# One PSUM bank for each partial product of a pair, down weights split ahead of the next pair's, turns one round later

## The chip, the cores and the metric

The kernel runs on one NeuronCore of a Trainium2 chip. The core has five engines that run side by side and meet at semaphores: TensorE (PE) multiplies matrices into PSUM, VectorE (DVE) and ScalarE (ACT) work on SBUF and PSUM, GpSimd (POOL) works on SBUF and issues some DMAs, SyncE (SP) issues most DMAs. PEld is PE's weight load, which overlaps its matmuls. Sixteen DMA engines move data between the main memory and SBUF.

The metric is the device time of one execution in microseconds (us).

## The reference

One layer of a diffusion backbone for 128 context tokens and 512 latent tokens, `D_MODEL` 1024, all in float32: modulation from a conditioning vector, RMS norm, one input projection shared by three mixers (neighbourhood attention, gated DeltaNet, gated linear attention), their merge and output projection, and a gated MLP with a centred convolution of width 3. The change touches the MLP alone:

```python
h2 = rms_norm(x, n2) * (1 + sc2) + sh2
u_val, u_gate = jnp.split(dw_conv(h2 @ w_up, f_conv), 2, axis=-1)
x = x + gt2 * ((jax.nn.silu(u_gate) * u_val) @ w_dn)
```

`w_up` is 1024 x 5632 and `w_dn` 2816 x 1024. The convolution doesn't cross from the latent to the context tokens.

## The kernel before, in words

Activations lie with features on the 128 partitions and the 640 tokens (T) side by side. A float32 matrix product is made of three passes: each operand is split into a high part (an ACT cast, L149 for weights, L402 for activations) and a low part (a DVE subtraction, L150 and L403), and high x high, high x low and low x high are added up in PSUM. `wh` and `wl` are rings of two tiles (`WB`), `whd` and `wld` for the down weights too; the raw weights that DMAs bring have a ring of three (`RAWB`), the raw down weights (`rawd`) of two.

PSUM is in three pools: `g`, two tiles of 1024 float32 a partition, two banks each (`gtile`); `m` and `s`, two tiles of 512, one bank each (`mtile`, `stile`).

The MLP's 22 hidden tiles of 128 features (f) come in six blocks of 4, 4, 4, 4, 3 and 3. The first block's are made plainly by `up_tile`: a value product (uv) and a gate product (ug), 48 matmuls of 320 columns each into a g tile, a convolution (`conv`: a centre tap on ACT, L510, and four side taps on DVE, L512), SiLU, a product, and a split into `ac[f]`. uv 0, ug 0 and uv 1 are made early, ahead of the normalisation. `sums_h2(k)` makes sums and differences of the activations' halves, which are split too (`hs`).

The other 18 tiles are made by `up_pair`. It makes value and gate together in the manner of Strassen and Winograd: the 2 x 2 block product (two halves of the input features, value and gate, two halves of the tokens, L and R) takes 7 products of 12 matmuls instead of 8. They build up in three partial sums, X, Y and Z, in the order X, Y, Z, X, Y, Z, Y. X and Y are the two banks of one g tile, Z is an s tile. Between two products into it, X is copied out by ACT (L1725 and L1741), and Y and Z are read by DVE (L1730, L1735, L1750, L1753, L1757).

The weights of a pair are four tiles, `("st", f, 0)` to `("st", f, 3)`. Some are sums of weight blocks: POOL's DMAs add one block onto another in the raw tile (L250), and DVE adds two raw tiles (`st_sums`, L264 for tile 0 and L267 for tile 2). L264 for the next pair needs both the next pair's weight 1 with its addition landed and the next pair's weight 0.

Behind each pair come two or three down projections of the block before (`down`): 24 matmuls (18 for a block of three) each, into g tiles, whose result DVE adds to the residual (L1782, two instructions). The down projections of the last block stand at the end, each followed by its turn: five transposes on PE (L617) into s tiles, two copies on ACT (L1790), two DMAs out on SP.

What sets the order: the stage of pairs and downs is under `tc.manual_schedule` for DVE, ACT and PE, so these engines run its instructions in the order in which the program issues them. Ahead of it, and on SP and POOL, a planner orders the instructions by readiness and priority. `W(key)` hands out a weight's split; for plain weights it loads two and splits one ahead (`LOOK_L`, `LOOK_S`), whatever the kind of the next. `need_split` and `need_load` issue a split or a load at their place.

At the end of a pair before the change the splits stand in this order: the first down weight's ahead of the last product; behind it the sum and split of the next pair's weight 0, the second down weight's split, and, ahead of the last down projection, that of the next pair's weight 1:

```python
        for i, key in enumerate(dn):
            if i == 0:
                st_sums(f + 1, 0)
                need_split(("st", f + 1, 0))
            if i + 1 < len(dn):
                need_split(dn[i + 1])
```

Of the kernel before, what the change touches and what calls it, by code (L numbers as in the profile page):

```python
# [18 lines left out]
P = 128  # L19
D = 1024  # L20
KT = 8
TS = 512
TP = 128
T = TS + TP
# [34 lines left out]
def hybrid_step(ctx: ExitStack, tc: tile.TileContext, a: dict, o: list):  # L59
# [18 lines left out]
    def gtile():  # L78
        return psg.tile([P, 1024], F32, tag="g", name=nm("g"))
# [4 lines left out]
    def stile():  # L84
        return psm.tile([P, 512], F32, tag="s", name=nm("s"))

    def body(ps):
        return ps[:, OFF:OFF + T]
# [197 lines left out]
    def need_split(key):  # L286
        j = pidx.get(key)
        if j is not None and j not in split:
            need_load(key)
            split[j] = split_of(j)  # L290

    def W(key):
        i = pidx[key]
        assert i == used[0], (key, i, used[0])
        used[0] += 1
        if key[0] in ("st", "wd"):
            need_split(key)
            return split[i]
        with tc.high_priority() if i else nullcontext():
            for j in range(i, min(i + LOOK_L + 1, len(plan))):  # L300
                if j not in loaded:
                    loaded[j] = load_of(j)
            for j in range(i, min(i + LOOK_S + 1, len(plan))):
                if j not in split:
                    split[j] = split_of(j)
        return split[i]

# [64 lines left out]
    def gemm_b(*args, **kw):  # L372
        for _ in gemm_p(*args, **kw):
            pass
# [1278 lines left out]
    def gated(f, uv, ug):  # L1653
# [3 lines left out]
        ac[f] = rt(2)  # L1657
        split_x(uv, *(t[:, :T] for t in ac[f]))

    def up_tile(f):  # L1660
        ys = {}

        for key, f2 in sorted((("uv", f), ("ug", NF + f)), key=lambda i: (i[0], f) in early):
            ys[key] = ft()
            if (key, f) in early:
                src = early[key, f]
            else:
                ps = gtile()
                gemm_b(ps, W((key, f)), lambda k: h2H[:, k, :], lambda k: h2L[:, k, :], KT)
                src = body(ps)  # L1670
            conv(ys[key], src, lambda tap, f2=f2: fcols[:, tap, f2:f2 + 1])
            if (key, f) in early:
                fslots.append(early[key, f])
        gated(f, ys["uv"], ys["ug"])
        fslots.extend(ys.values())

    L, R = slice(0, HALF), slice(HALF, T)
    hs = {}  # L1680

    def sums_h2(k):
# [21 lines left out]
    def up_pair(f, dn):  # L1704


        ps = gtile()
        X, Y, Z = ps[:, :HALF], ps[:, 512:512 + HALF], stile()[:, :HALF]

        def prod(out, w, kh, xx, start, stop):  # L1710

# [39 lines left out]
        prod(Z, w, 1, lambda j, k: hH2[j][:, 4 + k, R], False, True)  # L1751
        need_split(dn[0])
        V.tensor_add(u1[:, R], u1[:, R], Z)  # L1753
        w = W(("st", f, 3))
        prod(Y, w, 0, lambda j, k: hs[k, 1][j][:, L], False, True)
        open_["prev"] = f, conv_u(u1, f), u2
        V.tensor_sub(u2[:, L], Y, u2[:, L])  # L1757
        for i, key in enumerate(dn):
            if i == 0:
                st_sums(f + 1, 0)  # L1760
                need_split(("st", f + 1, 0))
            if i + 1 < len(dn):
                need_split(dn[i + 1])
            if i == len(dn) - 1:
                need_split(("st", f + 1, 1))
            down(*key[1:])
            need_load(*wds[wds.index(key) + 2:wds.index(key) + 3])
# [6 lines left out]
    def down(b, nt):  # L1774
        ps = gtile()
        if b == NB_F - 1:
            for n in (nt, nt + 1):
                need_split(("wd", b, n))
            need_load(("wd", b, nt + 2))
        gemm_b(ps, W(("wd", b, nt)), lambda k: ac[fst[b] + k][0], lambda k: ac[fst[b] + k][1], FBLK[b])  # L1780
        for r, (c0, c1) in enumerate(((0, TS), (TS, T))):
            V.scalar_tensor_tensor(out=x1[nt][:, c0:c1], in0=body(ps)[:, c0:c1], scalar=modc[:, 40 + nt, r:r + 1],  # L1782
                                   in1=x1[nt][:, c0:c1], op0=ALU.mult, op1=ALU.add)
        if nt == 7:
            for k in range(FBLK[b]):
                slots.extend(ac.pop(fst[b] + k))
        if b == NB_F - 1:
            yt_ = ft()
            yt = chunks(yt_)
            tr_chunks(x1[nt], lambda c0, n, v: S.copy(yt[:, c0:c0 + n, :], v))  # L1790
            ns_ = slice(nt * P, (nt + 1) * P)
            SY.dma_start(out=y_s[0, :, ns_].rearrange("(c p) d -> p c d", p=P), in_=yt[:, 0:4, :])
            SY.dma_start(out=y_p[0, :, ns_], in_=yt[:, 4, :])
            fslots.append(yt_)

    up_tile(1)
    up_tile(2)
    sums_h2(0)
    sums_h2(1)
    up_tile(0)  # L1800
    up_tile(3)
    sums_h2(2)
    sums_h2(3)
    e1x.close()
    e2 = ctx.enter_context(tc.tile_pool(name="e2", bufs=1, reuse_waits="tile"))
    slots.extend(e2.tile([P, T + 2], F32R, name=f"r{i}") for i in range(24, 32))
    with tc.manual_schedule(engines={nc.vector.engine, nc.scalar.engine, nc.tensor.engine}):
        need_load(*wds[:2])
        for b in range(1, NB_F):
            for i in range(FBLK[b]):  # L1810
                up_pair(fst[b] + i, [("wd", b - 1, nt) for nt in downs(b, i)])
        last_gate()
        for nt in range(8):
            down(NB_F - 1, nt)


# [32 lines left out]
```

## Time and profile before

| | |
|---|---|
| median of 3 runs | 1477.54 us (1476.49 to 1483.48) |
| profiled execution | 1470.56 us |
| its span, first to last instruction | 1468.3 us |
| PE busy | 1340.4 us (91%) |
| PEld busy | 1253.7 us (85%) |
| DVE busy | 900.4 us (61%) |
| ACT busy | 574.6 us (39%) |
| POOL busy | 218.1 us (15%) |
| mean granted TensorE clock | 0.972 of full speed |
| DMA | 137.96 MB, mean 94 GB/s |

All times in profile rows are of the one profiled execution, counted from its first instruction. A row of a group gives busy time, the mean duration of one instruction in ns, and the idle time of the engine just before such instructions with what ended most of it. A row in order of time gives start, duration, engine, line and operation, the tile written and those read (buffer numbers left out), and in brackets how long the engine had stood idle and what it waited for. Matmuls are pipelined, so the distance between two starts tells more than a duration. The up tiles run from about 936 to 979 us, the 18 pairs from 979.6, the last block's down projections from 1427.3.

### The profile page before, as it was taken

How to read it: one execution, taken by the hardware profiler on the slowest of the kernel's cores; microseconds unless marked ns; L12 is line 12 of the kernel's file. 1: busy time of each engine (PE TensorE's matmuls, PEld its weight loads, DVE VectorE, ACT ScalarE, POOL GpSimd, SP SyncE). 2: the span in 40 equal slices, each digit the busy share in tenths (PEclk: the TensorE clock that was granted, in tenths of full speed). 3: DMA queues.
4: the chain of work that ended last, by engine and by line, in shares of the span. 5: the costliest groups of instructions: out<-in, count | busy, mean ns of one | idle time of the engine just before them, and what ended most of it. 6: DMA issues, size and time to landing. Idle time of an engine off the chain costs nothing.

```text
span 1468.3 us, 27024 instructions
## 1 busy us (share of the span) xinstructions
PE 1340.4 (91%) x10985; PEld 1253.7 (85%) x10985; DVE 900.4 (61%) x1863; ACT 574.6 (39%) x1080; POOL 218.1 (15%) x224
## 2 busy tenths in 40 slices
PE   5999999998888999999999999888888898989886
PEld 4899999998777889999988989878888888888776
DVE  4775876676887543443433355886676666667663
ACT  4543334323855322343333245743333333332322
POOL 1011022212334110121200221001010101010100
PEclk9999999999999999999999999989999999999999
DMA  9524330331011344434445253115353444343413
GB/s 276 144 58 99 92 74 23 79 91 37 20 49 32 69 106 110 121 92 107 119 144 165 80 154 91 56 37 117 78 117 91 103 102 100 98 105 83 103 45 94
DMA packets 228078, 137.96 MB, mean 94 GB/s; under 512 B 22037, under 2 KB 221491, under 8 KB 227955
## 3 DMA queue, kind: packets, MB, share of 16 engines
q1 hardware_dynamic: 208563, 126.48, 31.5%
q0 software_dynamic: 19008, 9.44, 5.3%
q8 instruction: 86, 1.41, 0.4%
q14 instruction: 37, 0.30, 0.1%
q10 hardware_dynamic: 384, 0.33, 0.1%
HBM read 129.67 MB, written 6.55 MB: 93 GB/s over the span
## 4 chain that ended last, share of the span: by engine, by line
PE 61%; DVE 14%; ACT 6%; issue 4%; POOL 3%; DMA 1%; ACTq 0%; SPq 0%; DVEq 0%; POOLq 0%
PE g L369 34%; PE g L1714 9%; PE s L1714 4%; DVE t L512 3%; PE g L390 2%; ACT wh L149 2%; PE s L617 1%; DVE wl L150 1%; PE s L417 1%; PE s L1443 1%; ACT t L510 1%; DVE wld L150 1%; PE s L1431 1%; DVE raw L264 1%; POOL ssn L339 1%
## 5 line engine op out<-in xcount | busy, mean ns | idle before, releaser
L150 DVE TENSOR_TENSOR wl<-raw,wh 128x1024 fp32r<-128x1024 f32 (+1 forms) x176 | 193.6, 1100 | 193.5 <-ACT wh L149 182.5
L149 ACT CAST wh<-raw 128x1024 fp32r<-128x1024 f32 (+1 forms) x176 | 166.3, 945 | 343.7 <-PE g L369 176.5
L369 PE MATMUL g<-hH,wh 128*128 128x320 f32 x768 | 186.4, 322 | 3.0 <-DVE xb L725 1.5
L369 PE MATMUL g<-hL,wh 128*128 128x320 f32 x768 | 183.5, 317 | 0.6 <-DVE hL L465 0.6
L369 PE MATMUL g<-hH,wl 128*128 128x320 f32 x768 | 182.7, 316 | 0.0
L369 PE MATMUL g<-r,whd 128*128 128x320 f32 x704 | 145.4, 332 | 26.3 <-ACT whd L149 26.3
L369 PEld LDWEIGHTS g<-r,whd 128*128 128x128 f32 x704 | 120.1, 205 | 31.1 <-ACT whd L149 31.0
L369 PEld LDWEIGHTS g<-hH,wh 128*128 128x128 f32 x768 | 129.2, 191 | 11.2 <-issue 3.9
L369 PEld LDWEIGHTS g<-hL,wh 128*128 128x128 f32 x768 | 130.2, 190 | 3.4 <-issue 1.8
L369 PEld LDWEIGHTS g<-hH,wl 128*128 128x128 f32 x768 | 131.0, 191 | 2.2 <-issue 1.9
L1714 PE MATMUL g<-r,wh 128*128 128x320 f32 x432 | 100.3, 319 | 22.7 <-ACT t L1741 9.3
L250 POOL DMA_DIRECT2D raw<-in_w_up_dram x36 | 46.4, 1290 | 420.8 <-DMA raw<-in_w_up_dram 183.2
L1714 PEld LDWEIGHTS g<-r,wh 128*128 128x128 f32 x432 | 71.2, 188 | 32.8 <-ACT t L1741 14.0
L390 PE MATMUL g<-wh,hH 128*128 128x256 f32 x320 | 94.4, 295 | 3.4 <-DVE xb L725 3.4
L369 PE MATMUL g<-r,wld 128*128 128x320 f32 x352 | 88.1, 334 | 8.3 <-DVE wld L150 8.3
L512 DVE SCALAR_TENSOR_TENSOR t<-t,fcols,t 128x511 f32<-128x511 f32 (+1 forms) x156 | 82.2, 548 | 19.8 <-ACT t L510 17.3
L390 PE MATMUL g<-wl,hH 128*128 128x256 f32 x320 | 93.9, 293 | 0.0
L390 PE MATMUL g<-wh,hL 128*128 128x256 f32 x320 | 93.8, 293 | 0.0
L1782 DVE SCALAR_TENSOR_TENSOR xa<-g,modc,xa 128x512 f32<-128x512 f32 x96 | 48.3, 545 | 53.7 <-PE g L369 53.7
L369 PE MATMUL g<-oz,wh 128*128 128x320 f32 x384 | 73.8, 314 | 1.3 <-DVE xb L1304 1.2
L369 PEld LDWEIGHTS g<-r,wld 128*128 128x128 f32 x352 | 64.1, 206 | 12.7 <-DVE wld L150 12.7
L390 PEld LDWEIGHTS g<-wh,hH 128*128 128x128 f32 x320 | 62.6, 196 | 5.2 <-DVE xb L725 3.6
(594 smaller groups left out, 2912.4 us busy)
## 6 DMA issues: line engine op xcount, KB each, us to landing
raw<-in_w_in_dram SPq DMA_DIRECT2D x64, 512.0 KB
raw<-in_w_up_dram SPq DMA_DIRECT2D x90, 256.0 KB
wada<-in_w_ada_dram SPq DMA_DIRECT2D x32, 512.0 KB
raw<-in_w_up_dram POOLq DMA_DIRECT2D x36, 256.0 KB, 4.7
wat<-in_w_ada_dram SPq DMA_DIRECT2D x16, 512.0 KB
rawd<-in_w_down_dram SPq DMA_DIRECT2D x32, 256.0 KB
raw<-in_w_branch_dram SPq DMA_DIRECT2D x24, 256.0 KB
raw<-in_w_out_dram SPq DMA_DIRECT2D x8, 512.0 KB
```

Of the source, the lines that this page charges most:

```text
L149: S.copy(wh[:, :m], raw[:, :m])
L150: V.tensor_sub(wl[:, :m], raw[:, :m], wh[:, :m].bitcast(F32))
L250: G.dma_start(out=lo, in_=part(1, 2 - j), accum_op=ALU.add)
L264: V.tensor_add(st_raw[f, 0][:, 512:], st_raw[f, 0][:, :512], st_raw[f, 1][:, :512])
L339: G.tensor_tensor(out=out, in0=out, in1=mh.broadcast_to([P, n]), op=ALU.pow)
L369: PE.matmul(out=ps[:, OFF + c0:OFF + c1], lhsT=ww[:, k, :], rhs=xx(k)[:, c0:c1], start=(k == 0 and i == 0), stop=(k == kt - 1 and i == 2))
L390: PE.matmul(out=ps[b][:, o:o + GRP], lhsT=xx[:, 4 * kh + k, cs], rhs=ww[:, k, :], start=(kh == 0 and c % 2 == 0 and k == 0 and i == 0), st ...
L417: PE.matmul(out=pa[32 * g:32 * g + 32, :w], lhsT=csil[:, k, :], rhs=t[g], start=start, stop=stop)
L510: S.activation(out=y, in_=src, func=AF.Copy, scale=w3(1))
L512: V.scalar_tensor_tensor(out=y[:, o0:o1], in0=src[:, i0:i0 + o1 - o0], scalar=w3(t), in1=y[:, o0:o1], op0=ALU.mult, op1=ALU.add)
L1714: PE.matmul(out=out, lhsT=ww[:, 4 * kh + k, :], rhs=xx(hl_, k), start=start and k == 0 and i == 0, stop=stop and k == 3 and i == 2, skip_g ...
L1782: V.scalar_tensor_tensor(out=x1[nt][:, c0:c1], in0=body(ps)[:, c0:c1], scalar=modc[:, 40 + nt, r:r + 1], in1=x1[nt][:, c0:c1], op0=ALU.mul ...
```

## The change

X and Y of a pair become two m tiles, one bank each; g tiles are left to the down projections. The split of the second down weight is issued ahead of the pair's last product, and later down weights ahead of the next pair's. ug 2 is computed into two m tiles, half of the tokens each, and copied by ACT into an SBUF tile, from which its convolution reads. `W` no longer splits a pair's weight ahead; the split of `("st", 4, 0)` is issued behind ug 3's product. The order of up tiles and sums is changed, so that up tile 0 (whose products are early) stands last. The turns of the last block are a function of their own, issued one down projection later.

```diff
--- before.py
+++ after.py
@@ -301,7 +301,7 @@
                 if j not in loaded:
                     loaded[j] = load_of(j)
             for j in range(i, min(i + LOOK_S + 1, len(plan))):
-                if j not in split:
+                if j not in split and plan[j][0][0] != "st":
                     split[j] = split_of(j)
         return split[i]
 
@@ -1657,6 +1657,8 @@
         ac[f] = rt(2)
         split_x(uv, *(t[:, :T] for t in ac[f]))
 
+    L, R = slice(0, HALF), slice(HALF, T)
+
     def up_tile(f):
         ys = {}
 
@@ -1665,9 +1667,25 @@
             if (key, f) in early:
                 src = early[key, f]
             else:
-                ps = gtile()
-                gemm_b(ps, W((key, f)), lambda k: h2H[:, k, :], lambda k: h2L[:, k, :], KT)
-                src = body(ps)
+                w = W((key, f))
+                if (key, f) == ("ug", 2):
+
+                    ps = mtile(), mtile()
+                    for k in range(KT):
+                        for i, (ww, xx) in enumerate(((w[0], h2H), (w[0], h2L), (w[1], h2H))):
+                            for p_, cs in zip(ps, (L, R)):
+                                PE.matmul(out=p_[:, :HALF], lhsT=ww[:, k, :], rhs=xx[:, k, cs],
+                                          start=(k == 0 and i == 0), stop=(k == KT - 1 and i == 2))
+                    src = ft()
+                    for p_, cs in zip(ps, (L, R)):
+                        S.copy(src[:, cs], p_[:, :HALF])
+                    early[key, f] = src
+                else:
+                    ps = gtile()
+                    gemm_b(ps, w, lambda k: h2H[:, k, :], lambda k: h2L[:, k, :], KT)
+                    src = body(ps)
+                if (key, f) == ("ug", 3):
+                    need_split(("st", f + 1, 0))
             conv(ys[key], src, lambda tap, f2=f2: fcols[:, tap, f2:f2 + 1])
             if (key, f) in early:
                 fslots.append(early[key, f])
@@ -1676,7 +1694,6 @@
 
 
 
-    L, R = slice(0, HALF), slice(HALF, T)
     hs = {}
 
     def sums_h2(k):
@@ -1704,8 +1721,7 @@
     def up_pair(f, dn):
 
 
-        ps = gtile()
-        X, Y, Z = ps[:, :HALF], ps[:, 512:512 + HALF], stile()[:, :HALF]
+        X, Y, Z = mtile()[:, :HALF], mtile()[:, :HALF], stile()[:, :HALF]
 
         def prod(out, w, kh, xx, start, stop):
 
@@ -1751,16 +1767,17 @@
         prod(Z, w, 1, lambda j, k: hH2[j][:, 4 + k, R], False, True)
         need_split(dn[0])
         V.tensor_add(u1[:, R], u1[:, R], Z)
+        need_split(dn[1])
         w = W(("st", f, 3))
         prod(Y, w, 0, lambda j, k: hs[k, 1][j][:, L], False, True)
         open_["prev"] = f, conv_u(u1, f), u2
         V.tensor_sub(u2[:, L], Y, u2[:, L])
         for i, key in enumerate(dn):
+            if i + 1 < len(dn):
+                need_split(dn[i + 1])
             if i == 0:
                 st_sums(f + 1, 0)
                 need_split(("st", f + 1, 0))
-            if i + 1 < len(dn):
-                need_split(dn[i + 1])
             if i == len(dn) - 1:
                 need_split(("st", f + 1, 1))
             down(*key[1:])
@@ -1784,23 +1801,24 @@
         if nt == 7:
             for k in range(FBLK[b]):
                 slots.extend(ac.pop(fst[b] + k))
-        if b == NB_F - 1:
-            yt_ = ft()
-            yt = chunks(yt_)
-            tr_chunks(x1[nt], lambda c0, n, v: S.copy(yt[:, c0:c0 + n, :], v))
-            ns_ = slice(nt * P, (nt + 1) * P)
-            SY.dma_start(out=y_s[0, :, ns_].rearrange("(c p) d -> p c d", p=P), in_=yt[:, 0:4, :])
-            SY.dma_start(out=y_p[0, :, ns_], in_=yt[:, 4, :])
-            fslots.append(yt_)
+
+    def turn_out(nt):
+        yt_ = ft()
+        yt = chunks(yt_)
+        tr_chunks(x1[nt], lambda c0, n, v: S.copy(yt[:, c0:c0 + n, :], v))
+        ns_ = slice(nt * P, (nt + 1) * P)
+        SY.dma_start(out=y_s[0, :, ns_].rearrange("(c p) d -> p c d", p=P), in_=yt[:, 0:4, :])
+        SY.dma_start(out=y_p[0, :, ns_], in_=yt[:, 4, :])
+        fslots.append(yt_)
 
     up_tile(1)
+    sums_h2(0)
     up_tile(2)
-    sums_h2(0)
     sums_h2(1)
+    sums_h2(2)
+    up_tile(3)
+    sums_h2(3)
     up_tile(0)
-    up_tile(3)
-    sums_h2(2)
-    sums_h2(3)
     e1x.close()
     e2 = ctx.enter_context(tc.tile_pool(name="e2", bufs=1, reuse_waits="tile"))
     slots.extend(e2.tile([P, T + 2], F32R, name=f"r{i}") for i in range(24, 32))
@@ -1812,6 +1830,9 @@
         last_gate()
         for nt in range(8):
             down(NB_F - 1, nt)
+            if nt:
+                turn_out(nt - 1)
+        turn_out(7)
 
 
 # ---- launch: one core; inputs and outputs as the reference has them ----
```

## Rows read from the trace of the kernel before

**Rows 1.** The page of the kernel before: its first line, and from its part 4 (the chain of work that ended last) the shares of the span by engine.

```profile
span 1468.3 us, 27024 instructions
...
PE 61%; DVE 14%; ACT 6%; issue 4%; POOL 3%; DMA 1%; ACTq 0%; SPq 0%; DVEq 0%; POOLq 0%
```

**Rows 2.** The table by stretch: start and end in us, length, then busy us (and instructions) of PE, PEld (weight load), DVE, ACT and POOL, the granted TensorE clock, the share of the DMA engines and GB/s. The stretches are the first pair, the next eleven, the next three, the next two, the last pair with its down projections, and seven of the eight rounds at the end.

```profile
979.50:1009.50 30.00, 23.18 (x132) 21.56 (x133) 20.96 (x34) 11.79 (x17) 2.56 (x2) 0.89 0.36 79
1009.50:1273.50 264.00, 235.15 (x1454) 223.62 (x1453) 181.65 (x297) 91.11 (x132) 28.24 (x22) 0.95 0.45 99
1273.50:1351.10 77.60, 69.71 (x447) 66.57 (x446) 52.73 (x87) 25.89 (x38) 7.72 (x6) 0.98 0.43 97
1351.10:1399.20 48.10, 41.39 (x260) 39.30 (x259) 33.95 (x57) 16.54 (x25) 5.14 (x4) 0.96 0.44 98
1399.20:1421.00 21.80, 20.77 (x140) 20.19 (x138) 14.75 (x27) 6.57 (x11) 0.00 (x0) 1.00 0.14 40
...
1433.30:1463.50 30.20, 23.63 (x162) 22.03 (x162) 10.52 (x21) 7.75 (x20) 0.00 (x0) 1.00 0.37 103
```

**Rows 3.** What PE's matmuls waited for in the whole pair stage, 979 to 1413 us, each wait over 1 us in total: waiting engine, what it writes, line, what it waited for, us in total, times, longest.

```profile
PE g L369 <- ACT whd L149: 20.3, 17, 1.9
PE g L1714 <- ACT t L1741: 9.3, 18, 0.5
PE g L1714 <- ACT t L1725: 9.3, 18, 0.5
PE g L369 <- DVE wld L150: 8.3, 17, 0.5
PE g L1714 <- ACT r L402: 3.6, 1, 3.6
```

**Rows 4.** PE in order of time in one pair (start us, us, engine, line, operation, out<-in, shape, how many were merged, and in brackets the idle time before with what ended it): first matmul of X; first of Y after the copy of X; first and last matmul of X's second half; first of Y after the second copy; first of the first down projection; first of the second; its first with the low part; first matmul of the next pair.

```profile
1153.81 0.31 PE L1714 MATMUL g<-h2H,wh 128*128 128x320 f32 x1
...
1156.25 0.56 PE L1714 MATMUL g<-r,wh 128*128 128x320 f32 x2 [0.52 <-ACT t L1725]
...
1159.88 0.31 PE L1714 MATMUL g<-h2H,wh 128*128 128x320 f32 x1
...
1161.49 0.31 PE L1714 MATMUL g<-h2H,wl 128*128 128x320 f32 x1
1162.32 0.56 PE L1714 MATMUL g<-r,wh 128*128 128x320 f32 x2 [0.52 <-ACT t L1741]
...
1167.69 0.74 PE L369 MATMUL g<-r,whd 128*128 128x320 f32 x4
...
1172.46 0.85 PE L369 MATMUL g<-r,whd 128*128 128x320 f32 x4 [1.11 <-ACT whd L149]
1173.81 0.56 PE L369 MATMUL g<-r,wld 128*128 128x320 f32 x2 [0.49 <-DVE wld L150]
...
1176.83 0.31 PE L1714 MATMUL g<-h2H,wh 128*128 128x320 f32 x1
```

**Rows 5.** DVE in order of time in the same pair: the convolution of the pair before (L512), the second sum of weights (L267), the low part of weight 2, the convolution of this pair, the sum for the next pair (L264), the low part of the next pair's weight 0, the low part of the second down weight, and the result of the first down projection (L1782).

```profile
1154.94 2.18 DVE L512 SCALAR_TENSOR_TENSOR t<-t,fcols,t 128x511 f32<-128x511 f32 x4
1157.03 0.68 DVE L267 TENSOR_TENSOR raw<-raw,raw 128x512 f32<-128x512 f32 x1
...
1159.30 1.23 DVE L150 TENSOR_TENSOR wl<-raw,wh 128x1024 fp32r<-128x1024 f32 x1 [0.42 <-ACT wh L149]
...
1167.58 2.19 DVE L512 SCALAR_TENSOR_TENSOR t<-t,fcols,t 128x511 f32<-128x511 f32 x4 [0.96 <-ACT t L510]
...
1170.08 0.68 DVE L264 TENSOR_TENSOR raw<-raw,raw 128x512 f32<-128x512 f32 x1
1171.92 1.23 DVE L150 TENSOR_TENSOR wl<-raw,wh 128x1024 fp32r<-128x1024 f32 x1 [1.16 <-ACT wh L149]
1173.07 0.68 DVE L150 TENSOR_TENSOR wld<-rawd,whd 128x512 fp32r<-128x512 f32 x1
1173.67 1.00 DVE L1782 SCALAR_TENSOR_TENSOR xa<-g,modc,xa 128x512 f32<-128x512 f32 x2
```

**Rows 6.** ACT in order of time in the same pair: the copy of X, the centre tap of the convolution (L510), the cast of the next pair's weight 0, the cast of the second down weight.

```profile
1155.78 0.42 ACT L1725 COPY t<-g 128x320 f32<-128x320 f32 x1 [6.25 <-PE g L1714]
...
1166.71 0.83 ACT L510 ACTIVATE t<-t,fcols 128x640 f32<-128x640 f32 x1 [2.79 <-DVE t L1753]
1170.84 1.05 ACT L149 CAST wh<-raw 128x1024 fp32r<-128x1024 f32 x1 [3.30 <-DVE raw L264]
1171.80 0.61 ACT L149 CAST whd<-rawd 128x512 fp32r<-128x512 f32 x1
```

**Rows 7.** POOL and SP's queue in order of time in the same pair, the DMA that adds onto the next pair's weight 1 and the two loads of down weights (a merged row runs from the first issue to the end of the last); and, from the answer on line L250 in the whole stage, the time from issue to landing of its 34 additions.

```profile
1164.04 1.29 POOL L250 DMA_DIRECT2D raw<-in_w_up_dram  x1 [20.38 <-DVE wl L150]
...
1165.50 8.65 SPq L140 DMA_DIRECT2D rawd<-in_w_down_dram  x2
...
DMA to landing us min/median/max: 4.3/4.7/6.2
```

**Rows 8.** PE in order of time among the up tiles: the first matmul of ug2.

```profile
954.39 0.53 PE L369 MATMUL g<-h2H,wh 128*128 128x320 f32 x2 [4.25 <-DVE t L512]
```

**Rows 9.** DVE's waits from 950 to 992 us: the sum of weights for the first pair, which waited once.

```profile
DVE raw L264 <- DMA raw<-in_w_up_dram: 3.1, 1, 3.1
```

**Rows 10.** PE's groups from 1433.3 to 1463.5 us (busy us, mean ns of one, idle before and what ended it): the transposes of the turns.

```profile
L617 PE MATMUL s<-ident,xa 128*128 128x128 f32 x36 | 5.5, 280 | 7.4 <-DVE xa L1782 7.4
```

## The prediction

> **What bounds the kernel now.** I read the page first: the chain that ended last is 61% TensorE (PE), more than four times any other engine, in a span of 1468.3 us [rows 1]. So a cost counts where PE stands still. The table by stretch came next. In the eleven pairs from 1009.5 to 1273.5 PE is granted 0.95 of its clock and the DMA engines are used to 0.45; VectorE (DVE) works 181.65 of 264.0 us [rows 2]. Then the waits of PE for the whole pair stage: 20.3 us for the cast of a down weight (whd), 8.3 us for its low part (wld), and twice 9.3 us for ScalarE's (ACT's) copies at L1725 and L1741, eighteen times each [rows 3]. Last, one pair in order of time.
>
> In that pair a product of 12 matmuls runs at 1.61/11 = 0.1464 us a matmul (1159.88 to 1161.49), and the pair takes 1176.83 - 1153.81 = 23.02 us. It needs 7 x 12 + 2 x 24 = 132 matmuls, 19.3 us. The rest is four stops: each copy leaves 0.83 us between matmuls instead of 0.15 (1161.49 to 1162.32) and a slower first double (0.56), 0.78 us in all; the second down projection waits 1.11 us for whd and 0.49 us for wld, about 2.1 us with two restarts [rows 4]. [...]
>
> **The change part by part.**
>
> *X and Y in banks of their own.* Y's matmuls write other columns than the copy of X reads, yet they start only when the copy ends (0.52 us after PE ran dry, [rows 4]); from 1162.32 to 1167.69 three products, one of them in Z's own tile, run 36 matmuls in 5.37 us without a stop. So I take the wait to be one for the shared tile, and the new tiles to end it: 2 x 0.78 us a pair. What Y still needs (its own weights, the sums) is ready: rows 3, which holds every wait of PE over 1 us, has none for a wl. The m tiles come round once a pair; the last reader of the old Y is the subtraction just ahead of 1170.08 [rows 5], 6.7 us before the next X.
>
> *Down weights split earlier.* Now whd of the second down projection follows the cast of the next pair's first weight (1170.84), which waits 3.30 us for the sum L264, which waits for the convolution on DVE [rows 5, 6]. Moved ahead, its 0.61 us cast lies in ACT's 2.79 us of idle before L510 and its wld (0.68 us at 1173.07) in DVE's 0.96 us of idle before the convolution, so they cost nothing; without that cover 0.68 us a pair. Queued behind wld on DVE is the convolution, and the sum behind that. PE's 2.1 us stop goes. whd and wld are rings of two and the buffer's last user is a down projection of the pair before, so nothing is waited for.
>
> *What is late next.* Two down projections then run to 19.3 us after the pair's start; the next first weight's low part is ready at about 17.7 (1171.92 + 1.23 is 19.3 after the start now, less 1.6 for the two copies). PE isn't stopped there. But the weights come in a loop. The low part of weight 2 ends (1159.30 + 1.23 = 1160.53), which frees a raw buffer; SP loads it, POOL adds onto it at 1164.04, 3.5 us later, and the addition lands 4.3 to 6.2 us after that, median 4.7 [rows 5, 7]: 7.8 to 9.7 us. The sum starts at 1170.08, after 9.55 us, so it has hardly any slack today. Shortened by the stops it would be asked for after about 8.3. From the sum back to the low part of the next pair's weight 2 DVE and ACT need 3.0 (sum, cast, wl up to 1173.07) + 0.9 (down result) + 1.15 (wl) + 0.9 (down result) + 2.1 (convolution) + 0.7 (sum) + 1.1 (cast) + 1.25 (wl) = 11.1 us [rows 5, 6]. The loop is then 18.9 to 20.8 us against PE's 19.3. SP's second rawd load, now held until wld at 1173.75 and issued 8.65 us after the first was begun, will go out about 1 us after the first and so beside POOL's addition [rows 7]; I therefore take a landing of 5.7, not the median, a sum of 9.2 us, and a period of 20.3 us with a PE wait of about 1 us before the fifth product.
>
> [...]
>
> *Sum over the pairs.* Eleven pairs: 264.0 becomes 11 x 20.3 = 223.3, -40.7. The next three (132 + 156 + 156 matmuls, 77.6 us): 20.3 and twice 22.8 of PE work, which covers the loop, with 0.2 of waits: 66.3, -11.3. The two at 1351.1 (120 + 138 matmuls, 37.8 us of PE, less than the loop): the third down weight is split behind wl and a down result on DVE, 1 to 2 us late, and the loop adds as much: 41.3 against 48.1, -6.8. The last pair has only the two copies to lose, -1.5 [rows 2].
>
> *Up tiles, sums, split after ug3.* PE waits 4.25 us for a convolution to free a g tile before ug2 [rows 8]; two m tiles and two copies of 0.42 us [rows 6] end that. DVE stands 3.1 us for a DMA, at the sum that the look-ahead splits before ug3 [rows 9]; that goes. PE then waits 3.6 us for the last sums and runs the first pair at 0.89 of the clock, 30.0 us against 19.3 of work [rows 2, 3]. Both engines share the blame: DVE's own gain is 3.1 plus some of its later idle time, PE's cap is 10.7. The order before the pairs is a planner's, so a loss of 3 is possible too (up tile 0 left last, in front of the first pair's DVE work). I take -7, nearer PE's cap.
>
> *Late turns.* At the end each down projection is followed by 5 transposes that wait for DVE, 7.4 us together; 30.2 us for seven rounds [rows 2, 10]. With the turn of the round before put behind, the wait is covered by 18 matmuls (2.6 us) that need nothing from it: -7.5. The last turn waits as before. Bounds: 0 if the splits, queued behind the turn's copies on ACT, came late; 8.4 with the restarts.
>
> Sum: 40.7 + 11.3 + 6.8 + 1.5 + 7 + 7.5 = 74.8. The profiled execution took 1470.56 us (span 1468.3): 1395.8. The median shown is 1477.54, 7.0 above that: **1403 us**.
>
> **The rivals.**
>
> *The addition lands later.* With two rawd loads beside it, a landing 1.7 us later than I take (7.4, beyond the 6.2 seen) makes the period 22.0: 13 pairs x 1.7 = 22 more, 1425. For it: 6.2 was seen with one rawd load beside it [rows 7]; against: the DMA engines stand at 0.45 over the pair [rows 2]. 0.20.
>
> *The clock keeps falling.* The eleven pairs lose 13 us to it now [rows 2]; if the remaining 1 us stops still bring it down, the time is 1403 + 13 = 1416. Against it: from 1433.3 to 1463.5 PE stops about 1 us in every 4.3 and is granted 1.00 [rows 2, 10]. [...] 0.10.
>
> *The new tiles don't free PE from the copies.* If Y waits for the copy for another reason than the tile, 1.56 us a pair stay: 19.3 + 1.6 = 20.9, which hides most of the loop's wait; 0.6 x 13 + 1.5 = 9 more, 1412. For it: only that the trace can't show why the wait was set. 0.10.
>
> *Slower.* [...] The gains outside the loop are 34.1 us; 13 pairs must lose that and their own 45 as well, so the landing must grow by about 6 us, to 12, twice what was ever seen. Then some 1490. 0.03.
>
> **How the numbers follow.** My forecast holds 0.55, alone 1390 to 1415; the other cases stand as given, 0.02 is left over. Low end: loop no bound (-13) and transition at its cap (-4): 1386. High end: late landing with the lower gains before and after the pairs: 1432. A run of this kernel tells 0.5%, some 7 us, from no change: faster 0.95, within 0.02, slower 0.03.
>
> **What would show it.** Right: no PE wait for L1725, L1741 or whd in the pairs; pair starts 20 to 20.5 us apart; a wait of about 1 us for wl in the fifth product, and DVE's L264 waiting for a DMA; 3.2 us rounds at the end; granted clock near 1.00. Wrong: periods above 21.5, half-speed stretches between 1000 and 1270, or stops left at the copies. A first pair that starts no earlier than 979 would take the 7 away.

## The result and the profile after

The changed kernel takes **1412.68 us** (median of 4 runs, 1410.93 to 1417.0); the kernel before, run beside it, 1477.10. The ratio is 0.956, interval 0.952 to 0.959: faster by 64 us. Forecast were 1403 us, 1386 to 1432. The profiled execution took 1410.93 us. One run of the experiment with loads on ACT's queue (1453.83 us, at a clock of 0.84) was in a slow state and is left out of its time.

The rows below are from other kernels than those of the prediction, so their line numbers differ: in the changed kernel the products of a pair are L1730 (L1714 before), the two copies of X L1741 and L1757 (L1725 and L1741), the result of a down projection L1799 (L1782). Other kernels shift them by a few lines.

The page of the changed kernel: its first line, and from part 4 the shares of the chain that ended last, by engine:

```profile
span 1409.2 us, 27011 instructions
...
PE 52%; DVE 13%; DMA 11%; ACT 6%; issue 4%; POOL 3%; ACTq 0%; POOLq 0%; SPq 0%; DVEq 0%
```

PE was 61% of that chain and DMA 1% [rows 1]. Now DMA has 11%: the path to the end runs through transfers that it hardly ran through before. The table by stretch, columns and stretches as in [rows 2]; only the last line is cut otherwise, it is the rounds at the end from the first transpose to the last group:

```profile
975.40:1004.60 29.20, 24.18 (x133) 23.26 (x134) 24.46 (x42) 12.14 (x17) 2.56 (x2) 0.82 0.37 82
1004.60:1234.90 230.30, 219.89 (x1454) 213.66 (x1453) 176.80 (x295) 90.47 (x131) 28.23 (x22) 1.00 0.52 114
1234.90:1304.50 69.60, 66.52 (x446) 65.17 (x445) 54.73 (x91) 27.07 (x40) 7.71 (x6) 1.00 0.48 108
1304.50:1350.40 45.90, 40.94 (x261) 39.59 (x260) 33.51 (x57) 16.54 (x25) 5.14 (x4) 0.96 0.46 102
1350.40:1371.00 20.60, 20.43 (x139) 20.17 (x138) 14.80 (x28) 6.59 (x11) 0.00 (x0) 1.00 0.15 42
...
1383.90:1404.30 20.40, 19.83 (x145) 19.55 (x143) 9.87 (x19) 7.22 (x19) 0.00 (x0) 1.00 0.51 136
```

By these, with the starts of the pairs read from the trace:

| part of the span | before | after | change | forecast |
|---|---|---|---|---|
| up to the second pair | 1009.5 | 1004.6 | -4.9 | -7 |
| eleven pairs | 264.0 | 230.3 | -33.7 | -40.7 |
| next three | 77.6 | 69.6 | -8.0 | -11.3 |
| next two | 48.1 | 45.9 | -2.2 | -6.8 |
| last pair, to the first of the last downs | 28.05 | 26.5 | -1.55 | -1.5 |
| last downs and turns | 40.9 | 32.3 | -8.6 | -7.5 |
| span | 1468.3 | 1409.2 | -59.1 | -74.8 |

So every part gained, and the sum was 15.7 us too large. The medians differ by 5 us more than the spans, because the profiled execution of before lay 6.5 us under its median and that of after 1.75.

What PE waited for in the pair stage, 975 to 1371 us (columns as in [rows 3]):

```profile
PE m L1730 <- DVE wl L150: 14.2, 22, 1.5
PE m L1730 <- ACT wh L149: 3.1, 3, 1.8
PE g L369 <- DVE xa L1799: 2.5, 1, 2.5
```

The stops at the copies (18.6 us) and at whd and wld (28.6 us) of [rows 3] are gone. A new one stands at the low part of an up weight. Where it comes from, DVE's waits in the eleven pairs and the time from issue to landing of their 22 additions (L250) tell:

```profile
DVE raw L264 <- DMA raw<-in_w_up_dram: 23.0, 11, 3.3
...
DMA to landing us min/median/max: 5.0/5.9/6.9
```

In each of the eleven pairs the sum L264 waits for the addition, 2.1 us in the mean. Before, it waited for no DMA in any of them: by the trace the addition had landed 8.6 us after the low part of weight 2 in the mean, and the sum started after 9.56, behind DVE's convolution. That left 0.9 us of slack, where the prediction saw hardly any. One pair in order of time, the rows of PE, then DVE, POOL, SP's queue and ACT:

```profile
1066.61 0.31 PE L1730 MATMUL m<-h2H,wh 128*128 128x320 f32 x1
...
1075.54 0.41 PE L1730 MATMUL m<-r,wl 128*128 128x320 f32 x1 [0.70 <-DVE wl L150]
...
1080.65 0.75 PE L369 MATMUL g<-r,whd 128*128 128x320 f32 x4
...
1088.30 0.42 PE L1730 MATMUL m<-h2H,wh 128*128 128x320 f32 x1 [0.47 <-ACT wh L149]
...
1074.25 1.23 DVE L150 TENSOR_TENSOR wl<-raw,wh 128x1024 fp32r<-128x1024 f32 x1 [0.85 <-ACT wh L149]
...
1079.55 0.68 DVE L150 TENSOR_TENSOR wld<-rawd,whd 128x512 fp32r<-128x512 f32 x1
...
1086.43 0.69 DVE L264 TENSOR_TENSOR raw<-raw,raw 128x512 f32<-128x512 f32 x1 [3.26 <-DMA raw<-in_w_up_dram]
...
1079.47 1.28 POOL L250 DMA_DIRECT2D raw<-in_w_up_dram  x1 [17.35 <-DVE wld L150]
...
1079.26 1.36 SPq L140 DMA_DIRECT2D rawd<-in_w_down_dram  x2
...
1087.20 1.99 ACT L149 CAST wh<-raw 128x1024 fp32r<-128x1024 f32 x2 [6.65 <-DVE raw L264]
```

Here the two down weight loads go out within 1.36 us (in [rows 7] the second went out 8.65 us after the first), at the moment at which POOL issues its addition, and this addition lands 6.9 us later, at 1086.4. The sum follows it, ACT's cast follows the sum, and the next pair begins 21.69 us after this one. The loop that the prediction drew has two legs. The first, from the end of the low part of weight 2 to the start of L264, took 9.92 us in the mean of the eleven pairs (forecast 9.2, before 9.56). The second, the way back, took 11.21 or 11.22 in every one of them (forecast 11.1). Together that is 21.1; the starts of the pairs are 20.94 apart in the mean, as the first of the eleven begins with 2.2 us of slack that the others use up.

### The profile page after: what moved, and what is told of

Same layout as the page of the kernel before. It is cut to its first block, busy times and chain, and to the rows that moved or that the text cites. A ratio compares the mean times of both kernels' runs of the same rounds, so it can differ in the third digit from the quotient of the medians.

```text
span 1409.2 us, 27011 instructions
## 1 busy us (share of the span) xinstructions
PE 1322.5 (94%) x10985; PEld 1247.6 (89%) x10985; DVE 896.2 (64%) x1863; ACT 576.2 (41%) x1082; POOL 216.9 (15%) x224
## 4 chain that ended last, share of the span: by engine, by line
PE 52%; DVE 13%; DMA 11%; ACT 6%; issue 4%; POOL 3%; ACTq 0%; POOLq 0%; SPq 0%; DVEq 0%
PE g L369 34%; DMA raw<-in_w_up_dram 10%; PE g L390 4%; DVE wl L150 3%; ACT wh L149 3%; DVE t L512 2%; DVE xa L1799 2%; PE m L1730 2%; PE s L617 1%; PE s L417 1%; PE s L1443 1%; DVE raw L264 1%; PE s L1431 1%; POOL ssn L339 1%; DVE raw L267 1%
## 5 line engine op out<-in xcount | busy, mean ns | idle before, releaser
L369 PE MATMUL g<-r,whd 128*128 128x320 f32 x704 | 135.1, 314 | 10.1 <-ACT whd L149 6.1
L369 PEld LDWEIGHTS g<-r,whd 128*128 128x128 f32 x704 | 112.5, 192 | 11.0 <-ACT whd L149 6.3
L250 POOL DMA_DIRECT2D raw<-in_w_up_dram x36 | 46.4, 1290 | 369.1 <-DVE t L1766 191.4
L1730 PE MATMUL m<-r,wh 128*128 128x320 f32 x432 | 98.3, 314 | 0.5 <-DVE t L1766 0.5
L512 DVE SCALAR_TENSOR_TENSOR t<-t,fcols,t 128x127 f32<-128x127 f32 (+1 forms) x160 | 84.1, 548 | 9.4 <-ACT t L510 6.8
L369 PE MATMUL g<-r,wld 128*128 128x320 f32 x352 | 81.6, 313 | 0.0
L1730 PE MATMUL m<-r,wl 128*128 128x320 f32 x216 | 68.2, 316 | 7.9 <-DVE wl L150 7.9
L1730 PEld LDWEIGHTS m<-r,wh 128*128 128x128 f32 x432 | 72.0, 189 | 2.5 <-issue 0.6
L390 PEld LDWEIGHTS g<-wh,hL 128*128 128x128 f32 x320 | 64.1, 200 | 0.2 <-issue 0.2
```

The costliest lines, as they stand in the source:

```text
L250: G.dma_start(out=lo, in_=part(1, 2 - j), accum_op=ALU.add)
L369: PE.matmul(out=ps[:, OFF + c0:OFF + c1], lhsT=ww[:, k, :], rhs=xx(k)[:, c0:c1], start=(k == 0 and i == 0), stop=(k == kt - 1 and i == 2))
L390: PE.matmul(out=ps[b][:, o:o + GRP], lhsT=xx[:, 4 * kh + k, cs], rhs=ww[:, k, :], start=(kh == 0 and c % 2 == 0 and k == 0 and i == 0), st ...
L512: V.scalar_tensor_tensor(out=y[:, o0:o1], in0=src[:, i0:i0 + o1 - o0], scalar=w3(t), in1=y[:, o0:o1], op0=ALU.mult, op1=ALU.add)
L1730: PE.matmul(out=out, lhsT=ww[:, 4 * kh + k, :], rhs=xx(hl_, k), start=start and k == 0 and i == 0, stop=stop and k == 3 and i == 2, skip_g ...
```

## The experiments

Each ratio is to the kernel before, run on the same chip in the same series. "Period" is the mean distance of the first matmuls of the eleven pairs. The kernel before took 1475.1 to 1478.8 us in the four series, so differences of a few microseconds between series tell little.

### One part of the change undone

**X and Y back in one g tile.**

```diff
-        X, Y, Z = mtile()[:, :HALF], mtile()[:, :HALF], stile()[:, :HALF]
+        ps = gtile()
+        X, Y, Z = ps[:, :HALF], ps[:, 512:512 + HALF], stile()[:, :HALF]
```

> The changed kernel with X and Y back in one g tile; all else stays. Theory (the loop through the landing of POOL's addition sets the pair's period, 11.2 us from the sum L264 back to weight 2's low part, plus 9.9 us to the next sum): the two stops of 0.78 us at the copies come back but eat the slack that PE now loses in waiting for low parts, so the eleven pairs from the second go from 20.9 to 21.0-21.6 us each, and the time from 1412.7 to 1413-1424. Rival (the parts simply add): 18 x 1.56 = 28 us come back, 1441.

1411.0 us, 0.955 (0.951 to 0.959): as fast as the whole change. PE's waits in the eleven pairs, their stretch, and the landing of their additions:

```profile
PE g L1731 <- ACT t L1742: 5.7, 11, 0.5
PE g L1731 <- ACT t L1758: 5.7, 11, 0.5
...
1000.80:1231.70 230.90, 219.56 (x1455) 213.78 (x1454) 181.04 (x298) 91.22 (x132) 28.24 (x22) 1.00 0.51 113
...
DMA to landing us min/median/max: 4.6/5.2/5.8
```

The tile is what set the wait: with one tile both stops are back, 0.5 us each. But the period is 20.98, against 20.94 without them. Here PE sets it: 132 x 0.1464 + 2 x 0.78 = 20.9, and L264 waits for no DMA. In the changed kernel PE needs 19.3, and the late addition fills the rest up to 20.9. Two different bounds stand at the same height.

**Down weights split in the old order.**

```diff
-        need_split(dn[1])
         w = W(("st", f, 3))
...
         for i, key in enumerate(dn):
-            if i + 1 < len(dn):
-                need_split(dn[i + 1])
             if i == 0:
                 st_sums(f + 1, 0)
                 need_split(("st", f + 1, 0))
+            if i + 1 < len(dn):
+                need_split(dn[i + 1])
```

> The changed kernel with the second down weight split again behind the next pair's weight 0. Theory: the stop of about 2.1 us at the second down projection comes back, but the second rawd load goes out 8 us later again, so the addition lands after 8.5-9.0 instead of 9.9 us; period 21.4-22.2, time 1420-1436, with some half-speed stretches between 1000 and 1270 again. Rival (parts add): 2.1 x 16 plus the clock's 13 come back, 1459.

1453.63 us, 0.984 (0.981 to 0.987): 41 us of the 64 are lost, more than I expected. PE's waits in the eleven pairs, DVE's, and their stretch:

```profile
PE g L369 <- ACT whd L149: 20.6, 11, 2.4
PE g L369 <- DVE wld L150: 5.3, 11, 0.5
...
DVE raw L264 <- DMA raw<-in_w_up_dram: 8.0, 11, 1.3
...
1008.90:1268.70 259.80, 233.88 (x1454) 228.03 (x1454) 180.61 (x297) 91.11 (x132) 28.24 (x22) 0.93 0.46 101
```

The first leg is 9.17 us, the way back 14.45 instead of 11.22, the period 23.62: their sum. The stop at whd lies *in* the loop. It follows the cast that waits for the sum; the second down projection follows it, DVE's two result instructions follow that, and the next convolution, sum and cast queue behind them on DVE and ACT. So to split early doesn't take a stop of PE away beside the loop, it shortens the loop, by 3.2 us in all. Part of that is the clock: the one pair of the eleven that was granted 1.00 took 22.03 us with a way back of 13.1, the others, at 0.93, 23.5 to 24.2 us with 14.4 to 14.7. Of the 3.2 us some 1.9 are thus the order and the rest the clock.

**Old front** (the up tiles, the sums, ug 2 in a g tile and the look-ahead split).

```diff
-                if j not in split and plan[j][0][0] != "st":
+                if j not in split:
...
-                if (key, f) == ("ug", 2):
+                if False:
...
-                if (key, f) == ("ug", 3):
-                    need_split(("st", f + 1, 0))
```

and the calls of `up_tile` and `sums_h2` in their old order.

> The changed kernel with the old order of up tiles and sums, ug 2 in a g tile and the look-ahead split. Theory: the second pair starts 5 us later, as before the change, and all behind it is as in the changed kernel: 1418 (1415-1421). Rival (this part brought nothing, the gain at the front came from the banks): 1413.

1414.82 us, 0.958 (0.954 to 0.962). The second pair starts at 1008.66, 4.1 us later than with the change, but the eleven pairs then ran at 20.50 instead of 20.94, with additions that landed a little earlier in this execution (5.4 us in the median for 5.9). The medians are 2.1 us apart and the intervals overlap, so what the front is worth in time isn't settled.

**Old turns.**

```diff
-            if nt:
-                turn_out(nt - 1)
-        turn_out(7)
+            turn_out(nt)
```

> The changed kernel with each turn right behind its down projection. Theory: seven rounds of 4.3 instead of 3.18 us, 8 us come back: 1420.5 (1419-1422). Rival (the rounds are now bound by the loads of down weights or the copies on ACT): under 4 us.

1418.60 us, 0.960 (0.957 to 0.963), 5.9 us above the changed kernel, with intervals that overlap a little. The transposes' wait over the end of this kernel, and their group in the changed one (1383.9 to 1404.3 us):

```profile
PE s L617 <- DVE xa L1799: 7.4, 8, 0.9
```

```profile
L617 PE MATMUL s<-ident,xa 128*128 128x128 f32 x35 | 5.0, 272 | 0.0
```

7.4 us of waiting come and go with the order alone; the rounds are 4.31 us apart here, as before, and 3.18 in the changed kernel.

### The disputed landing by itself

**No additions in the pairs** (what is left out stands in the expectation).

```diff
-        if j in (1, 2):
+        if j in ():
```

> The changed kernel without POOL's two additions a pair: weights 1 and 2 of a pair lack one of their summands, so two 256 KB transfers a pair are left out. Theory (the landing of the addition sets the period): L264 no longer waits for a DMA, it comes when DVE asks for it, 8.3 us after weight 2's low part; the eleven pairs go from 20.9 to 19.4-19.7 us, the time to 1386-1394. Rival (DVE's ordered work sets the period, the landing only coincides): pairs stay above 20.5 us, 1408-1413.

1387.22 us, 0.941 (0.936 to 0.945). The eleven pairs:

```profile
1002.30:1216.00 213.70, 213.70 (x1454) 213.70 (x1453) 178.57 (x298) 91.20 (x132) 0.00 (x0) 1.00 0.33 96
```

PE is busy in all of the stretch: 213.7/11 = 19.43 a pair, 0.1 above its own work. Without the addition nothing else holds a pair of two down projections.

**Only the first two down weights loaded** (left out as the expectation says).

```diff
+            old = mlp.setdefault("old", [])
+            if len(old) > 1:
+                old.append(old[-2])
+                return old[-1]
```

> The changed kernel in which all down projections use the first two down weights that were loaded; the other loads of down weights are left out, the splits stay. Theory (the two rawd loads, now one behind the other, lengthen the addition's flight from 5.1 to 6.0 us): flight 4.3-4.7 us, sum 8.3-8.6 us after weight 2's low part, pairs 19.4-19.9 us, time 1388-1400. Rival (the flight is longer because the up weights' own loads stand closer together): flight stays 5.5-6 us, pairs 20.5-21, 1408-1413.

1389.79 us, 0.942 (0.940 to 0.944). Landing of the additions and the eleven pairs:

```profile
DMA to landing us min/median/max: 4.2/4.5/5.3
...
1005.60:1221.60 216.00, 214.73 (x1454) 213.65 (x1453) 178.95 (x298) 91.84 (x132) 28.24 (x22) 1.00 0.45 95
```

The additions stay, and land 1.4 us earlier in the median. The period is 19.64.

**The down weights' loads on ACT's queue**, nothing left out.

```diff
-            SY.dma_start(out=rv[:, :, c0:c0 + cn], ...
+            (S if down else SY).dma_start(out=rv[:, :, c0:c0 + cn], ...
```

> The changed kernel with the loads of down weights issued on ACT's queue, where the order written out puts them behind the casts of the next pair's weights, instead of on SP, where they go out as soon as the buffer is free. Nothing is left out. Theory: they no longer run beside the first addition; flight 4.3-4.8 us, pairs 19.4-20.0 us, time 1392-1402. Rival (the up weights' own loads make the flight long): no change in flight, and two issues a pair on ACT cost 0-0.8 us a pair: 1412-1425.

1394.61 us (three runs), 0.945 (0.943 to 0.947). The same two answers:

```profile
DMA to landing us min/median/max: 4.2/4.5/4.8
...
1006.50:1223.10 216.60, 215.14 (x1455) 213.84 (x1454) 178.99 (x298) 91.67 (x132) 28.24 (x22) 1.00 0.54 121
```

The same bytes, at other times and from another queue: ACT reaches the two loads 8.6 to 11 us after the low part of weight 2, when the first addition has landed; SP sends them out after 3.8 and 4.8 us, just as that addition is issued. The first leg falls to 8.47 us, the way back stays at 11.22, and the period is 19.68. So the delay is the two loads *beside* the addition, not the additions or the loads as such. It cost 18 us of the changed kernel. Whether another queue alone, at the old times, would help wasn't tried.

### The way back, and one part alone

**Sum L267 and the copy of X moved ahead of the gate's convolution**, the convolution ahead of the second product into Y; its loads stay on SP.

```diff
+        S.copy(u2[:, L], X)
+        need_split(("st", f, 1))
+        st_sums(f, 2)
...
-        S.copy(u2[:, L], X)
-        need_split(("st", f, 1))
...
-        st_sums(f, 2)
```

> The changed kernel with the sum L267 ahead of the gate's convolution on DVE, and the convolution ahead of the product Y; nothing is left out. Theory: the cast of weight 2 then runs beside the convolution instead of behind it; the way back in the loop goes from 11.2 to about 10.3 us, pairs from 20.9 to 20.0-20.4, time 1398-1405. Rival (DVE's total work sets the period): its order moves nothing, 1411-1414.

1396.07 us, 0.945 (0.942 to 0.948). DVE's wait in the eleven pairs, and their stretch:

```profile
DVE raw L264 <- DMA raw<-in_w_up_dram: 14.2, 11, 2.3
...
1009.30:1225.20 215.90, 215.10 (x1453) 213.69 (x1453) 177.69 (x298) 92.86 (x132) 28.24 (x22) 1.00 0.54 121
```

The sum still waits for the addition in every pair, but the way back is now 10.28 to 10.88 us and the loop fits beside PE: period 19.63. An edit of the other leg thus gives nearly the same gain, which fits the loop as the bound. But it isn't the other leg alone: the first leg fell too, from 9.92 to 9.13 us, about half of what the loop lost. Why the additions landed earlier here (5.0 us in the median for 5.9) isn't shown.

**Before, with the early split alone** (the edit above, in the other direction).

> The kernel before with the down weights split ahead of the next pair's and nothing else of the change: X and Y stay in one g tile. Theory (this part alone opens the loop, the banks bring nothing while the landing is late): pairs 20.9-21.1 us with two stops of 0.78 us at the copies, no wait for whd, L264 hardly waits for a DMA; front and end as before; 1429-1437. Rival (the parts add, the banks are needed for it): pairs above 21.8, over 1442.

1427.61 us, 0.967 (0.963 to 0.970): 49 us come from the place of the down weights' splits alone. Waits and stretch of the eleven pairs:

```profile
PE g L1714 <- ACT t L1725: 5.7, 11, 0.5
PE g L1714 <- ACT t L1741: 5.7, 11, 0.5
...
1013.60:1243.40 229.80, 218.48 (x1454) 212.69 (x1453) 180.98 (x298) 91.16 (x132) 28.23 (x22) 1.00 0.52 114
```

Period 20.89, PE's 20.9 with its two copies once more; and the clock is 1.00 with both stops still there.

**Before, with the two m tiles alone.**

> The kernel before with X and Y in two m tiles and nothing else of the change. Theory: the stops at the copies go, but the second down weight's cast still waits for the sum L264, which now waits for the landing; PE stands there instead; pairs 23.4-23.9 instead of 24.0 us, time 1466-1475. Rival (the two stops of 0.78 us a pair simply go): 28 us, 1448.

1466.53 us, 0.993 (0.991 to 0.996), 10 us. The wait at whd grows into what the copies left. First the line of the kernel before for its eleven pairs, then this kernel's, with DVE's wait:

```profile
PE g L369 <- ACT whd L149: 12.1, 11, 1.2
```

```profile
PE g L369 <- ACT whd L149: 20.8, 11, 2.4
...
DVE raw L264 <- DMA raw<-in_w_up_dram: 7.8, 11, 1.2
...
1008.60:1267.20 258.60, 233.17 (x1454) 227.11 (x1453) 180.60 (x297) 91.10 (x132) 28.24 (x22) 0.93 0.45 101
```

Two stops of 0.78 us were taken out of each pair, and the period fell by 0.49, to 23.51: 0.8 us came back at whd, as the sum now waits for the addition in every pair, and the clock fell from 0.95 to 0.93. The loop, not PE's own work, sets the period.

### What follows, put together

**Loads on ACT's queue, X and Y in one g tile.**

> The changed kernel with the loads of down weights on ACT's queue, and X and Y back in one g tile. Theory (with the landing out of the way PE's own work sets the period, so here the banks are worth their 1.56 us a pair): pairs 20.8-21.1 instead of 19.7 us, time 1409-1418. Rival (the banks are worth nothing anywhere): 1392-1398 as with separate banks.

1415.88 us, 0.959 (0.957 to 0.962):

```profile
1009.70:1240.50 230.80, 219.48 (x1454) 213.69 (x1453) 180.54 (x298) 91.19 (x132) 28.24 (x22) 1.00 0.51 113
```

With the landing out of the way the banks are worth 1415.9 - 1394.6 = 21 us; with it they are worth nothing (1411.0 against 1412.7). The two tiles pay only once the loop has room.

**Loads on ACT's queue and the order of the experiment on the way back**, with all of the change.

> The changed kernel with the loads of down weights on ACT's queue and the sum L267 ahead of the gate's convolution; nothing is left out. Theory: all pairs at PE's 19.4-19.5 us, the third to fifth too, which the landing still held at 20.2-20.6 with either edit alone; some 3-6 us under the better of the two, 1386-1393. Rival (both edits buy the same slack and the rest is elsewhere): 1393-1397.

1389.85 us (1388.77 to 1392.66), 0.942 (0.940 to 0.945):

```profile
1002.70:1217.40 214.70, 214.43 (x1455) 213.68 (x1454) 178.64 (x298) 92.62 (x132) 28.23 (x22) 1.00 0.54 122
```

The additions land after 4.7 us in the median, PE waits 0.3 us over the eleven pairs together, the period is 19.52, and this is the fastest kernel that does all of the work: 23 us below the changed one. Over the shift of the loads alone the second edit adds 5 us in the medians, but the intervals overlap, so this isn't settled. PE's 19.3 is nearly reached.

## Why the prediction was right, and where not

**Right: what goes.** In the pair stage no wait of PE for the copies or whd is left, for the reasons given: the tile set the copies' wait (one tile brings it back), and the early split found its cover. Right too: the next bound is the loop through POOL's addition, the wait is at the fifth product (0.70 us in the pair shown; PE's waits for low parts make up 9.6 us in the eleven pairs) with DVE's L264 ahead of it, and SP's second load goes out 1 us after the first.

**Mis-sized: the landing.** The step that failed is "I therefore take a landing of 5.7, not the median, a sum of 9.2 us". The first addition of a pair was issued 3.9 us after the low part of weight 2 in the mean, where I had 3.5, and landed 6.0 us later, up to 6.9, where I had 5.7; the sum came after 9.92, and each pair took 20.94 - 20.3 = 0.64 us more: 7 us in the eleven. So the pairs don't start 20 to 20.5 us apart, as I had said they would. The size isn't a firm one: in the kernels with the old front and the old turns, whose pairs are the same, the first leg was 9.47 and 9.73 us in the mean. Of the range given for the loop, 18.9 to 20.8, I took a point near the middle of its upper half where the upper end belonged: that stood nearest to the 20.94 measured. The runs show that an addition lands later with loads beside it, 5.9 us in the median with two (the changed kernel) against 4.5 with none (their loads on ACT's queue); how a load delays it they don't show. In the pair shown, from 1079 to 1087 us, two queues carried the weights, SP's with 0.76 MB and POOL's with 0.51. The rival of the late addition was thus half true: the place and the loads beside the addition, but 0.64 us a pair instead of 1.7.

**Mis-sized: the pairs with three down projections.** I priced the next three at 66.3 us and the next two at 41.3; 69.6 and 45.9 were measured. PE's two long stops there, from the trace of the changed kernel in order of time:

```profile
1277.67 0.83 PE L369 MATMUL g<-r,whd 128*128 128x320 f32 x4 [1.33 <-ACT t L510]
...
1346.13 1.12 PE L369 MATMUL g<-r,whd 128*128 128x320 f32 x4 [2.54 <-DVE xa L1799]
```

Both are the third down projection of a pair. It needs the g tile of the first, as the g ring has two, and DVE's result (L1799) frees that tile. DVE's rows ahead of the second stop:

```profile
1341.98 0.69 DVE L264 TENSOR_TENSOR raw<-raw,raw 128x512 f32<-128x512 f32 x1 [1.46 <-DMA raw<-in_w_up_dram]
...
1344.97 1.00 DVE L1799 SCALAR_TENSOR_TENSOR xa<-g,modc,xa 128x512 f32<-128x512 f32 x2
```

The result stands behind the next pair's sum, which waits for the late addition, and behind that pair's first low part. It ended at 1345.97, and PE went on at 1346.13; ACT had cast the third down weight by 1344.2. At the first stop the result ended at 1277.52, next to the ACT instruction that the row names. So a stop is still there once a pair, now at the tile. I had 1 to 2 us, for the third weight's split, in the two pairs of 48.1 us, and left it out for the three before them ("which covers the loop, with 0.2 of waits"). Without additions two such pairs take 22.88 us each, PE's own work. In the fastest kernel that does all of the work these pairs still take 24.07, 23.66 and 25.27 us; an earlier third split or a third g tile wasn't tried.

**What the list of stops couldn't tell: what a part is worth alone.** By the durations of [rows 4] and the clock of [rows 2] the eleven pairs before the change are 1452 x 0.1464 = 212.6 us of matmuls, 22 x 0.78 = 17 of stops for the copies, 11 x 2.1 = 23 of stops for whd and wld, and 264 x (1 - 0.95) = 13 for the clock: 266 for the 264.0 measured. Where the loop had room, these prices held: the early split alone took the eleven pairs from 264.0 to 229.8 us, 34 for the 36 counted with the clock; with the loads on ACT's queue the two tiles take them from 230.8 to 216.6, 14 for 17. But the parts don't add. The early split is worth 41 to 49 us of the whole time, the tiles alone 10, and beside the split nothing while the additions land late. Before the change the sum had 0.9 us of slack to the landing; the tiles take 1.56 us out of a pair, more than that, and 0.8 us comes back as a longer stop at whd, which stands behind the sum. The list of waits [rows 3] can't show that: it has a stop of PE that follows the sum and one that doesn't in the same form. What could have told it is to go on from whd's cast around the loop once, which I did only for the order after the change.

**The time that a wrong rival had.** "The new tiles don't free PE from the copies" was given 20.9 us a pair and 1412 us, and 1412.7 was measured. It is false all the same: PE is free of the copies. A kernel with them (1411.0) and one without (1412.7) are equally long, and only the rows tell them apart.

**The clock.** Before, half-speed stretches are in the trace, as 0.50 from 1031.5 to 1033.5 us. After the change the clock is 1.00 over the eleven pairs, with 16 stops of at most 0.7 us for low parts (9.6 us in all), and over the next three, and the 13 us came back as forecast. The rival of a falling clock doesn't hold there. Over the next two pairs it is 0.96: after the stop of 2.54 us shown above 0.68 is granted, from 1345 to 1350.4 us.

**Front, last pair, turns.** The front gave 4.9 us in the trace for 7 forecast (the first pair still runs at 0.82 of the clock), and no gain that the runs can tell; the last pair 1.55 for 1.5; the turns 8.6 for 7.5 in the trace, 5.9 in the medians.

## What to carry to other kernels

When a stop of the busy engine goes, follow its releaser all the way around, through the DMA that refills the buffer, before adding stops up: in this kernel a stop inside such a loop lengthened every pair, one beside it cost nothing until the loop was shorter than the engine's own work. A transfer on a loop's path needs its time taken with the neighbours that it will have after the change; here two loads that a removed stop let out early cost 18 us, and sending the same loads from another queue, later, gave it back. Two edits that each seem worth nothing, or the same, may hide behind one bound: test one again when the other is in place.

## What the hardware showed unexpectedly

- An addition of 256 KB by POOL's DMA takes 4.5 to 4.7 us from issue to landing (medians of four kernels) with no down weight load beside the first addition of a pair, 4.7 to 4.9 with one (three kernels), and 5.0 to 5.9 (medians of six, up to 6.9 for one addition) with two of 256 KB in flight, although the DMA engines are used only to 0.52 in the mean over the changed kernel's pairs.
- Two stops of 0.5 us in each pair of 21 us go with a granted clock of 1.00 (three kernels: 20.89 to 20.98 us a pair); one of 1.9 us in the mean at whd with 0.5 more at wld goes with 0.93 (two kernels), and one of 1.1 us at whd with the other three of 0.5 with 0.95 (the kernel before).
- The same stops don't always bring the clock down: in the kernel before, four of the eleven pairs ran at 1.00 and took 23.0 to 23.1 us, seven at 0.93 and took 24.55, each with the same four stops. The pair that the prediction read is one of the four.
